# Spatial gating g of a two-layer encoder step starts with U(g+1) instead of U(g), and its first loads are issued during VM

## The chip, the core and the metric

The kernel runs on one core of a Trainium2 chip. The metric is the device time of one execution in microseconds (us). The engines are TensorE (PE, its weight loads PEld), VectorE (DVE), ScalarE (ACT) and SyncE (SP, which here issues every DMA). GpSimd (POOL) does nothing that matters.

## The reference, cut to what matters

Each of the two layers normalises x, multiplies it by one combined matrix `w_in`, and feeds two branches: retention (q, k, v, gr) and a gated MLP (u, vm, gm). Only the second matters here. There are 288 tokens: 256 of a prompt and 32 of a sample.

```
z = rmsnorm(x) @ w_in
q, k, v, gr, u, vm, gm, ar, am = split(z)
u  = gelu(u)
vn = layernorm(gelu(vm), ln_g, ln_b)          # over all 2048 channels: needs the whole of vm
s  = einsum(W_s, vn) + bias                   # per group of 256 channels, mixes positions
m_branch = (silu(gm) * u * s) @ w_mlp_out
merged = sigmoid(ar) * r_branch + sigmoid(am) * m_branch
x = x + merged @ w_o
```

## The kernel before

**Jobs and pieces.** Every projection is cut into jobs of 256 output channels, and a job into four pieces (`KP` = 4 k-tiles of 128 x 256 weights, 512 KB). All operands are split into a high and a low fp32r part, and a product takes three matmuls (`mm3`, lines 111 to 113), so that a piece is 4 x 2 x 3 = 24 matmuls. A layer has 88 jobs: first eight of VM (pieces 0 to 31 of the layer), then, before the change, U0, GM0, U1, GM1 ... U7, GM7 (pieces 32 to 95), then AM0, AM1, W_MLP0 and so on. Below, "piece 42" or "step 42" counts within a layer.

**What a step emits.** The order on every engine is the order in which the main loop (line 769) writes the instructions; nothing reorders them later. At step s it emits the high part of piece s+4 (`emit_hi`: ACT, tile `whi`, 5 buffers), the low part of piece s+3 (`emit_lo`: DVE, tile `wlo`, 4 buffers, so that DVE can write it only when PE has finished piece s-1), the load of piece s+7 (`emit_raw`: SP, tile `raw`, 4 buffers), the job's `pre` function if it is a first piece, the 24 matmuls, and then one `tick()`. A tick advances every active generator by one `yield`: the evacuations (`evac_*`, started after the last piece of their job) and the spatial gatings (`sgu_gen`, started in `pre`). I call the tick of step 37 "tick 37".

**Spatial gating.** `sgu_gen(l, g)` waits until the layer norm's statistics are there (`state["ln"]`, written in tick 37 by the last VM evacuation). Then, tick by tick: it clears a part of `wr` (DVE, line 292, which needs that matrix loaded) and normalises one of three token blocks of `vmt` (tile `vmacc`, lines 299 and 301), ACT takes the high part of the matrix (tile `wsp`, one buffer); then DVE takes the low parts and does the other two blocks; then ACT writes `vh`, and SP gets the store `out_gv` and, through `load_sgu`, the five loads of gating g+1 (480 KB: `ln_g`, `ln_b`, `ws_b`, `ws`, `ws_s`); then DVE writes `vl` and the low part of `vh` (line 108); then PE does ten matmuls (lines 324 to 326), and DVE adds the bias and multiplies by u (lines 328 to 332, tile `rqh`). `evac_gm(g)` multiplies the result by silu(gm). The loads of gating 0 are issued by gating 0's own first step, at piece 32.

Before the change gating 0 starts with U0 at piece 32 but waits for the statistics, and gating 1 starts with U1 at piece 40; so the two run side by side from tick 40 on.

Of the kernel before, what the change touches and what calls it, by code (L numbers as in the profile page):

```python
# [23 lines left out]
NPR = DM // 256  # L24
# [6 lines left out]
Q0, K0, V0, GR0, U0, VM0, GM0, AR0, AM0 = 0, 4, 8, 16, 24, 32, 40, 48, 56  # L31
# [11 lines left out]
def trunk(ctx: ExitStack, tc: tile.TileContext, a, o):  # L43
# [9 lines left out]
    def st(shape, tag, dt=F32, bufs=1):  # L53
        return sb.tile(shape, dt, tag=tag, name=tag, bufs=bufs)

    def aux():
        return psx.tile([P, 512], F32, tag="aux", name="aux")
# [19 lines left out]
    def load(dst, src):  # L77
        nc.sync.dma_start(out=dst, in_=src)  # L78
# [25 lines left out]
    def to_hi(src, hi):  # L104
        S.copy(out=hi, in_=src)  # L105

    def to_lo(src, hi, lo):
        V.tensor_tensor(out=lo, in0=src, in1=hi.bitcast(F32), op=ALU.subtract)  # L108
# [125 lines left out]
    def halves2(p):  # L234
        return p.rearrange("p (j c) -> p j c", j=2)
# [31 lines left out]
    def load_sgu(l, g):  # L267
        if g == NPR:
            return
        lg, lb = st([P, 416], "c0", bufs=2)[:, 0:256], st([P, 256], "c1", bufs=2)  # L270
        load(lg, a["ln_g"][l, g].partition_broadcast(P))
        load(lb, a["ln_b"][l, g].partition_broadcast(P))
        bs = st([P, 384], "wh", bufs=2)[:, 0:T]
        load(bs, a["ws_b"][l, g].partition_broadcast(P))
        wr = st([P, P], "wsr", bufs=2)
        load(wr, a["ws"][l, g])
        wq = st([P, TS], "wsq", bufs=2)
        load(wq, a["ws_s"][l, g])
        state["sgu", g] = (lg, lb, bs, wr, wq)

    def sgu_gen(l, g):
        if g == 0:
            load_sgu(l, 0)
        lg, lb, bs, wr, wq = state.pop(("sgu", g))
        while "ln" not in state:
            yield
        if g == 0:
            yield
        vmt, r = state["vmt"], state["ln"]
        if g == NPR - 1:  # L290
            state.pop("ln")
        V.memset(wr[64:128, 0:64], 0.0)
        w2 = st([P, 2, P], "wsp", F32R)
        to_hi(wr, w2[:, 0])
        wsk = st([P, TS], "wsk", F32R, bufs=2)
        to_hi(wq, wsk)
        for b in range(3):
            x = vmt[:, g, :, b]
            V.scalar_tensor_tensor(out=x, in0=x, scalar=mvl[:, b, 0:1], in1=halves2(lg),  # L299
                                   op0=ALU.subtract, op1=ALU.mult)  # L300
            V.scalar_tensor_tensor(out=x, in0=x, scalar=r[:, b:b + 1], in1=halves2(lb),
                                   op0=ALU.mult, op1=ALU.add)
            if b == 0:
                yield
                to_lo(wr, w2[:, 0], w2[:, 1])
                for q in ODD:
                    to_lo(wq[q], wsk[q], wsk[q])
        yield
        vh, vl = st([P, 2, 3, P], "vh", F32R, bufs=2), st([P, 2, 2, P], "vl", F32R, bufs=2)
        to_hi(vmt[:, g], vh)  # L310
        load(halves2(o["gv"][l, :, g * 256:g * 256 + 256]), vmt[0:TS, g, :, 2])
        load_sgu(l, g + 1)
        yield
        to_lo(vmt[:, g, :, 0:2], vh[:, :, 0:2], vl)
        to_lo(vmt[HALF, g, :, 2], vh[HALF, :, 2], vh[HALF, :, 2])
        yield
        while ("u", g) not in state:
            yield
        sg = st([P, 2, T], "rqh")
        ps_ = aux()  # L320
        for d in range(2):
            p = aux().rearrange("p (b h i) -> p b h i", b=2, h=2)
            for b in range(2):
                PE.matmul(p[:, b], vh[:, d, b], w2, start=True, stop=False)  # L324
                PE.matmul(p[:, b, 0], vl[:, d, b], w2[:, 0], start=False, stop=True)  # L325
            PE.matmul(ps_[:, d * TS:d * TS + TS], vh[:, d, 2], wsk, start=True, stop=True)
            x = sg[:, d, 0:TP].rearrange("p (b i) -> p b i", b=2)
            V.tensor_tensor(out=x, in0=p[:, :, 1], in1=bs[:, 0:TP].rearrange("p (b i) -> p b i", b=2), op=ALU.add)  # L328
            V.tensor_tensor(out=x, in0=p[:, :, 0], in1=x, op=ALU.add)
        V.tensor_tensor(out=sg[:, :, TP:T], in0=ps_[:, 0:2 * TS].rearrange("p (d i) -> p d i", d=2),  # L330
                        in1=bs[:, TP:T].unsqueeze(1).to_broadcast([P, 2, TS]), op=ALU.add)
        V.tensor_tensor(out=sg, in0=sg, in1=state.pop(("u", g)), op=ALU.mult)
        state["s", g] = sg

    def evac_u(l, g, ps):
        z = scaled(ps, "zu", 2)
        S.activation(out=z, in_=z, func=AF.Gelu)
        yield
        state["u", g] = z
# [280 lines left out]
    for l in range(DEPTH):  # L620
        A, B = ("A", "B") if l % 2 == 0 else ("B", "A")
        hs, mg, rg, mr = Set(A), Set(B), Set(B), Set(A)
        sets[l] = (hs, mg, rg, mr)

        def job(pair, ops, fn, c, pre=None, l=l):
            jobs.append((l, pair, ops, fn, c, pre))

        for c in range(NPR):
            job(VM0 + c, hs, evac_vm, c)
        for g in range(NPR):  # L630
            job(U0 + g, hs, evac_u, g, lambda l, g: start(sgu_gen(l, g)))
            job(GM0 + g, hs, evac_gm, g)
        job(AM0, hs, evac_am, 0)
        for c in range(NPR):
            if c + 1 < NPR:
                job(AM0 + c + 1, hs, evac_am, c + 1)
            job(W_MLP + c, mg, evac_mlp, c)
        for hp in range(H // 2):
            job(Q0 + hp, hs, evac_q, hp, pre_q)
            job(K0 + hp, hs, evac_k, hp)  # L640
            for jj in range(2):
                job(V0 + 2 * hp + jj, hs, evac_v, 2 * hp + jj)
            for jj in range(2):
                job(GR0 + 2 * hp + jj, hs, evac_gr, 2 * hp + jj)
        for c in range(NPR):
            job(AR0 + c, hs, evac_ar, c)
        for c in range(NPR):
            job(W_RET + c, rg, evac_ret, c)
        for c in range(NPR):
            job(W_O + c, mr, evac_o, c, pre_o)  # L650
# [39 lines left out]
    def start(gen):  # L690
        active.append(gen)
# [77 lines left out]
    for s, (j, i) in enumerate(pieces):  # L769
        l, pair, ops, fn, c, pre = jobs[j]  # L770
# [6 lines left out]
        if i == 0:  # L777
# [5 lines left out]
            hs, mg, rg, mr = sets[l]  # L783
# [133 lines left out]
```

## Time and profile before

| what | us |
|---|---|
| median of three runs | 2361.43 |
| lowest, highest | 2360.75, 2362.48 |
| the profiled execution, own time | 2362.0 |
| its span (first to last instruction) | 2360.2 |
| PE busy | 2335.9 (99%) |
| DVE busy | 1424.1 (60%) |
| ACT busy | 1020.2 (43%) |
| mean granted TensorE clock | 0.995 |

PE is busy nearly all the time, so that a change of order can only win or lose the stretches in which PE waits, or in which it runs at the lower of its two clock levels. The rows are to be read with the engine that waits first, and what it waited for second.

### The profile page before, as it was taken

To read this page: it belongs to the slowest core of one execution; us is meant where nothing else is said; L and a number is where in the kernel's file an instruction comes from. 1 tells how busy PE (TensorE), PEld (TensorE's weight loads), DVE (VectorE), ACT (ScalarE), POOL (GpSimd) and SP (SyncE) were. 2 spreads that over 40 slices of the span, in tenths; PEclk is the share of its full clock that TensorE was granted. 3 is DMA by queue.
4 is the path that set the end of the run, shared out by engine and by line. 5 is a ranking of instruction groups with operands and counts; after the bars stand their busy time and mean duration, and the time that the engine had idled before them with its cause. 6 is when DMAs were issued, how large, how long until landed. Compare 5 with 4: busy or idle time off the path is not lost.

```text
span 2360.2 us, 42693 instructions
## 1 busy us (share of the span) xinstructions
PE 2335.9 (99%) x17572; PEld 2333.9 (99%) x17572; DVE 1424.1 (60%) x2145; ACT 1020.2 (43%) x1298; POOL 0.2 (0%) x4
## 2 busy tenths in 40 slices
PE   9999999999999999999999999999999999999997
PEld 9999999999999999999999999999999999999997
DVE  7567764446777774455555777544467777645554
ACT  6445543333444453334444445433344444433342
POOL 0000000000000000000000000000000000000000
PEclk9999999999999999999999999999999999999999
DMA  8855554556778785456688555445577877744553
GB/s 268 234 171 180 175 173 163 168 165 185 219 206 230 201 223 173 163 168 193 210 218 229 165 176 177 163 163 168 172 203 198 222 206 212 219 164 162 169 196 115
DMA packets 350164, 446.36 MB, mean 189 GB/s; under 512 B 193552, under 2 KB 254736, under 8 KB 349968
## 3 DMA queue, kind: packets, MB, share of 16 engines
q1 hardware_dynamic: 349968, 443.63, 62.1%
q8 instruction: 138, 2.26, 0.4%
q14 instruction: 58, 0.48, 0.1%
HBM read 412.09 MB, written 31.46 MB: 188 GB/s over the span
## 4 chain that ended last, share of the span: by engine, by line
PE 96%; DVE 2%; issue 1%; DMA 1%; SPq 0%; ACT 0%; DVEq 0%; ACTq 0%
PE ps L111 31%; PE ps L112 31%; PE ps L113 31%; PE aux L112 1%; PE aux L113 1%; PE aux L111 1%; DMA raw<-in_w_in 1%; PE aux L324 0%; DVE wlo L108 0%; DMA vmacc<-zd 0%; SPq L78 0%; PE aux L325 0%; DVE vmacc L825 0%; DVE vmacc L299 0%; PE aux L423 0%
## 5 line engine op out<-in xcount | busy, mean ns | idle before, releaser
L108 DVE TENSOR_TENSOR wlo<-raw,whi 128x1024 fp32r<-128x1024 f32 (+1 forms) x705 | 858.0, 1218 | 509.3 <-PE ps L113 321.5
L105 ACT CAST whi<-raw 128x1024 fp32r<-128x1024 f32 (+1 forms) x705 | 733.2, 1047 | 817.8 <-PE ps L112 659.1
L111 PE MATMUL ps<-Ah,whi 128*128 128x288 f32 x2816 | 832.6, 296 | 1.4 <-ACT whi L105 1.4
L113 PE MATMUL ps<-Ah,wlo 128*128 128x288 f32 x2816 | 832.0, 295 | 0.7 <-DVE wlo L108 0.7
L112 PE MATMUL ps<-Al,whi 128*128 128x288 f32 x2816 | 831.2, 295 | 0.0
L111 PE MATMUL ps<-Bh,whi 128*128 128x288 f32 x2784 | 825.2, 296 | 0.0
L112 PE MATMUL ps<-Bl,whi 128*128 128x288 f32 x2784 | 823.8, 296 | 0.0
L113 PE MATMUL ps<-Bh,wlo 128*128 128x288 f32 x2784 | 823.8, 296 | 0.0
L111 PEld LDWEIGHTS ps<-Ah,whi 128*128 128x128 f32 x2816 | 529.8, 188 | 1.9 <-ACT whi L105 1.9
L113 PEld LDWEIGHTS ps<-Ah,wlo 128*128 128x128 f32 x2816 | 529.3, 188 | 1.4 <-DVE wlo L108 1.4
L112 PEld LDWEIGHTS ps<-Al,whi 128*128 128x128 f32 x2816 | 529.1, 188 | 0.0
L112 PEld LDWEIGHTS ps<-Bl,whi 128*128 128x128 f32 x2784 | 524.4, 188 | 0.0
L111 PEld LDWEIGHTS ps<-Bh,whi 128*128 128x128 f32 x2784 | 523.9, 188 | 0.0
L113 PEld LDWEIGHTS ps<-Bh,wlo 128*128 128x128 f32 x2784 | 523.4, 188 | 0.0
L209 DVE TENSOR_TENSOR z<-ps,rsb 128x576 f32<-128x576 f32 x52 | 39.3, 755 | 61.7 <-PE ps L113 61.7
L512 ACT ACTIVATE on<-aux,gnb,gny 128x256 f32<-128x256 f32 x48 | 23.6, 562 | 65.4 <-DVE gnb L508 65.4
L216 DVE STREAM_TRANSPOSE zt<-ps 128x512 f32<-128x512 f32 x32 | 22.9, 715 | 39.8 <-PE ps L113 38.2
L503 DVE BATCH_NORM_STATS2 gst<-aux 128x6 f32<-128x256 f32 x48 | 17.5, 421 | 34.5 <-PE aux L113 34.5
L355 ACT ACTIVATE z<-z 128x576 f32<-128x576 f32 x16 | 11.0, 687 | 46.3 <-DVE z L209 46.3
L384 DVE TENSOR_TENSOR zu<-ps,cosr 128x576 f32<-128x576 f32 x16 | 12.1, 758 | 30.6 <-PE ps L113 30.6
L375 DVE TENSOR_TENSOR vmacc<-ps,z 128x576 f32<-128x576 f32 x16 | 12.1, 758 | 30.6 <-PE ps L113 30.6
L328 DVE TENSOR_TENSOR rqh<-aux,wh 128x256 f32<-128x256 f32 x32 | 13.4, 419 | 27.8 <-PE aux L325 27.8
(221 smaller groups left out, 1146.1 us busy)
## 6 DMA issues: line engine op xcount, KB each, us to landing
raw<-in_w_in SPq DMA_DIRECT2D x511, 512.0 KB, 4.7
raw<-in_w_mlp SPq DMA_DIRECT2D x64, 512.0 KB, 4.6
raw<-in_w_ret SPq DMA_DIRECT2D x64, 512.0 KB, 4.6
raw<-in_w_o SPq DMA_DIRECT2D x64, 512.0 KB, 4.6
zd<-zt SPq DMA_DIRECT2D x224, 96.0 KB, 3.7
vmacc<-zd SPq DMA_DIRECT2D x56, 384.0 KB, 5.8
c<-in_dmask SPq DMA_DIRECT2D x16, 208.0 KB, 4.8
vmacc<-in_x SPq DMA_DIRECT2D x8, 288.0 KB, 6.8
```

The source lines that it names most:

```text
L105: S.copy(out=hi, in_=src)
L108: V.tensor_tensor(out=lo, in0=src, in1=hi.bitcast(F32), op=ALU.subtract)
L111: PE.matmul(out, lh, rh, start=start, stop=False)
L112: PE.matmul(out, lh, rl, start=False, stop=False)
L113: PE.matmul(out, ll, rh, start=False, stop=stop)
L209: V.tensor_tensor(out=z, in0=ps[:, :, 0:T], in1=bc2(state["rs"]), op=ALU.mult)
L216: V.transpose(out=zt[:, :, 0:8], in_=src[:, :, 0:TP].rearrange("p j (b t) -> p j b t", t=TS))
L328: V.tensor_tensor(out=x, in0=p[:, :, 1], in1=bs[:, 0:TP].rearrange("p (b i) -> p b i", b=2), op=ALU.add)
L375: V.tensor_tensor(out=state["acc"][:, c], in0=ps[:, :, 0:T], in1=state.pop(("sig", c)), op=ALU.mult)
L384: V.tensor_tensor(out=r, in0=ps[:, :, 0:T], in1=bc2(cr), op=ALU.mult)
L503: V.bn_stats(out=bst[:, b], in_=src[b])
L512: S.activation(out=on[:, b], in_=src[b], func=AF.Identity, bias=nb[:, b:b + 1], scale=y[:, b:b + 1])
```

## The change

Gating g now starts in the `pre` of U(g+1) (gating 7 in that of GM7); the jobs stand in the order U0, U1, GM0, U2, GM1, ... U7, GM6, GM7, so that U1 has pieces 36 to 39, GM0 40 to 43 and U2 44 to 47. The five loads of gating 0 are issued in the `pre` of VM5 (piece 20) instead of at piece 32.

```diff
     def sgu_gen(l, g):
-        if g == 0:
-            load_sgu(l, 0)
         lg, lb, bs, wr, wq = state.pop(("sgu", g))
...
+    def pre_vm(l, c):
+        if c == 5:
+            load_sgu(l, 0)
+
+    def start_sgu(l, g):
+        if g:
+            start(sgu_gen(l, g - 1))
...
         for c in range(NPR):
-            job(VM0 + c, hs, evac_vm, c)
+            job(VM0 + c, hs, evac_vm, c, pre_vm)
         for g in range(NPR):
-            job(U0 + g, hs, evac_u, g, lambda l, g: start(sgu_gen(l, g)))
-            job(GM0 + g, hs, evac_gm, g)
+            job(U0 + g, hs, evac_u, g, start_sgu)
+            if g:
+                job(GM0 + g - 1, hs, evac_gm, g - 1)
+        job(GM0 + NPR - 1, hs, evac_gm, NPR - 1, lambda l, g: start_sgu(l, NPR))
         job(AM0, hs, evac_am, 0)
```

What this moves on the engines, at three places of layer 0 (layer 1 has the same rows). In the listings a row is a line of the program, an operation, and output<-inputs; line numbers above 280 differ between the two kernels by a few.

DVE, from the evacuation after piece 39 on. Before: `z` is GM0's result, the first `wlo` is that of step 40, the MEMSET and the two rows under it (with the tiles `c_1676`, `c_1677`) are the start of gating 1, the second `wlo` is that of step 41, and `vl`, `vh` are gating 0's low parts.

```order
L209 TENSOR_TENSOR z<-ps,rsb 128x576
L108 TENSOR_TENSOR wlo<-raw,whi 128x1024
L292 MEMSET wsr 64x64
L299 SCALAR_TENSOR_TENSOR vmacc<-vmacc,mvl,c_1676 128x2x128
L301 SCALAR_TENSOR_TENSOR vmacc<-vmacc,lny,c_1677 128x2x128
L108 TENSOR_TENSOR wlo<-raw,whi 128x1024
L108 TENSOR_TENSOR vl<-vmacc,vh 128x512
L108 TENSOR_TENSOR vh<-vmacc,vh 64x2x128
```

The same place on DVE in the changed kernel (`zu` is U1's result).

```order
L209 TENSOR_TENSOR zu<-ps,rsb 128x576
L108 TENSOR_TENSOR wlo<-raw,whi 128x1024 x2
L108 TENSOR_TENSOR vl<-vmacc,vh 128x512
L108 TENSOR_TENSOR vh<-vmacc,vh 64x2x128
L108 TENSOR_TENSOR wlo<-raw,whi 128x1024
L326 TENSOR_TENSOR rqh<-aux,wh 128x256
```

The three rows of gating 1 no longer stand ahead of gating 0's `vl` and `vh`; they now stand behind gating 0's bias and product rows, in step 44. On PE, gating 0's ten matmuls stand at the same place as before, behind piece 42; gating 1's stand behind piece 48 instead of piece 45.

ACT, from the high part of piece 43 (step 39) on, before: `z` is GM0's silu, and the `wsp`, `wsk` rows are gating 1's.

```order
L105 CAST whi<-raw 128x1024
L343 ACT_TABLE_LOAD
L343 ACTIVATE z<-z 128x576
L105 CAST whi<-raw 128x1024
L105 CAST vh<-vmacc 128x768
L105 CAST wsp<-wsr 128x128
L105 CAST wsk<-wsq 128x32
L105 CAST whi<-raw 128x1024 x2
```

The same place on ACT in the changed kernel: `zu` is U1's gelu.

```order
L105 CAST whi<-raw 128x1024
L343 ACTIVATE zu<-zu 128x576
L105 CAST whi<-raw 128x1024
L105 CAST vh<-vmacc 128x768
L105 CAST whi<-raw 128x1024 x3
L349 ACT_TABLE_LOAD
L349 ACTIVATE z<-z 128x576
```

Gating 1's `wsp` moved behind GM0's silu, and U1's gelu follows U0's without a table load between them. Over the program, ACT's table loads for gelu and silu of U and GM go from 30 to 26.

SP, from the four stores of VM4's transposed result (`zd<-zt`) on, before.

```order
L78 DMA zd<-zt 32x24x32 x4
L78 DMA raw<-in_w_in 128x1024 x2
L78 DMA vmacc<-zd 128x6x128
L78 DMA raw<-in_w_in 128x1024 x2
```

The same place on SP in the changed kernel.

```order
L78 DMA zd<-zt 32x24x32 x4
L78 DMA raw<-in_w_in 128x1024
L78 DMA c_937<-in_ln_g 128x256
L78 DMA c_938<-in_ln_b 128x256
L78 DMA wh<-in_ws_b 128x288
L78 DMA wsr<-in_ws 128x128
L78 DMA wsq<-in_ws_s 128x32
L78 DMA raw<-in_w_in 128x1024
L78 DMA vmacc<-zd 128x6x128
```

The five loads moved here from the same position three jobs later (behind VM7's stores and one `raw`).

## Rows read from the trace of the kernel before

**Rows 1.** The page: the span, and busy time, share and instructions by engine.

```profile
span 2360.2 us, 42693 instructions
PE 2335.9 (99%) x17572; PEld 2333.9 (99%) x17572; DVE 1424.1 (60%) x2145; ACT 1020.2 (43%) x1298; POOL 0.2 (0%) x4
```

**Rows 2.** Waits of PE: who waited for whom, total us, times, longest.

```profile
PE aux L325 <- DVE vl L108: 9.0, 2, 5.6
```

**Rows 3.** Timeline of PE, layer 0: start, duration, instruction, [idle before <-releaser].

```profile
146.92 0.28 PE L324 MATMUL aux<-wsp,vh 128*128 128x256 f32 x1
152.77 0.47 PE L325 MATMUL aux<-wsp,vl 128*128 128x128 f32 x1 [5.57 <-DVE vl L108]
...
157.72 0.30 PE L111 MATMUL ps<-Ah,whi 128*128 128x288 f32 x1
...
165.68 0.28 PE L324 MATMUL aux<-wsp,vh 128*128 128x256 f32 x1
...
168.42 0.30 PE L111 MATMUL ps<-Ah,whi 128*128 128x288 f32 x1
...
192.32 0.28 PE L324 MATMUL aux<-wsp,vh 128*128 128x256 f32 x1
```

**Rows 4.** Timeline of PE, layer 1, the same place.

```profile
1314.96 0.28 PE L324 MATMUL aux<-wsp,vh 128*128 128x256 f32 x1
1318.67 0.47 PE L325 MATMUL aux<-wsp,vl 128*128 128x128 f32 x1 [3.42 <-DVE vl L108]
...
1325.07 0.30 PE L111 MATMUL ps<-Bh,whi 128*128 128x288 f32 x1
```

**Rows 5.** Windows: us, busy (instructions) by engine, granted clock, DMA share, GB/s.

```profile
60.00:100.00 40.00, 40.00 (x303) 40.00 (x303) 21.13 (x29) 17.12 (x22) 0.00 (x0) 1.00 0.92 248
152.80:157.70 4.90, 4.90 (x21) 4.90 (x22) 2.81 (x9) 2.31 (x4) 0.00 (x0) 0.50 0.31 107
1318.70:1325.00 6.30, 6.30 (x27) 6.30 (x28) 4.21 (x10) 2.32 (x4) 0.00 (x0) 0.50 0.25 83
```

**Rows 6.** Timeline of DVE: layer 0, gating 2 of layer 0, layer 1.

```profile
129.25 1.23 DVE L108 TENSOR_TENSOR wlo<-raw,whi 128x1024 fp32r<-128x1024 f32 x1 [2.55 <-ACT whi L105]
...
141.25 1.22 DVE L108 TENSOR_TENSOR wlo<-raw,whi 128x1024 fp32r<-128x1024 f32 x1
149.83 0.11 DVE L292 MEMSET wsr<- 64x64 f32 x1 [7.36 <-DMA wsr<-in_ws]
...
152.03 0.68 DVE L108 TENSOR_TENSOR vl<-vmacc,vh 128x512 fp32r<-128x512 f32 x1
152.74 0.42 DVE L108 TENSOR_TENSOR vh<-vmacc,vh 64x256 fp32r<-64x256 f32 x1
...
184.87 0.42 DVE L108 TENSOR_TENSOR vh<-vmacc,vh 64x256 fp32r<-64x256 f32 x1
...
1315.72 0.11 DVE L292 MEMSET wsr<- 64x64 f32 x1 [6.51 <-DMA wsr<-in_ws]
```

**Rows 7.** Timeline of ACT: layer 0, then layer 1.

```profile
141.96 1.04 ACT L105 CAST whi<-raw 128x1024 fp32r<-128x1024 f32 x1
142.90 0.83 ACT L105 CAST vh<-vmacc 128x768 fp32r<-128x768 f32 x1
154.82 0.30 ACT L105 CAST wsp<-wsr 128x128 fp32r<-128x128 f32 x1 [11.09 <-PE aux L325]
...
1308.71 1.03 ACT L105 CAST whi<-raw 128x1024 fp32r<-128x1024 f32 x1
1309.64 0.83 ACT L105 CAST vh<-vmacc 128x768 fp32r<-128x768 f32 x1
```

**Rows 8.** Timeline of SP's queue: the load of gating 1's matrix.

```profile
144.81 0.38 SPq L78 DMA_DIRECT2D wsr<-in_ws  x1
```

**Rows 9.** Chain that ended last, in order of time: start, us, what.

```profile
118.58 9.49 DMA raw<-in_w_in
```

**Rows 10.** Groups by line, ACT: xcount, busy us, mean ns, idle before.

```profile
L343 ACT ACT_TABLE_LOAD x16 | 20.5, 1283 | 0.3
```

## The prediction

> **What bounds the kernel now.** I read the page first: PE is busy 2335.9 of 2360.2 us [rows 1], so nothing that DVE, ACT or SP win counts unless PE waits for it. Next the waits of PE: the longest by far is on the low part `vl` in front of a spatial gating's matmuls, 9.0 us in two waits [rows 2]. The timeline of PE puts them at gating 0 of each layer: it comes to the gating's first matmul at 146.92 and to the one that reads `vl` only at 152.77, idle 5.57 us [rows 3]; in layer 1 the wait is 3.42 us [rows 4]. The other fourteen gatings show none.
>
> The wait is dearer than its idle time. Behind both waits the windows show a granted clock of 0.50, for 4.9 and 6.3 us [rows 5]: the engine had sat idle, and then ran at 1.2 GHz instead of 2.4.
>
> Who made `vl` late? On DVE the low part of piece 43 starts at 141.25 and takes 1.22 us. Then DVE stands at gating 1's MEMSET until 149.83, waiting 7.36 us for that gating's matrix [rows 6], whose load SP had issued only at 144.81 [rows 8]. `vl` is queued behind it and comes at 152.03. ACT had `vh` ready at 142.90 + 0.83 = 143.73 [rows 7], so DVE alone was late. ACT too stood still there, 11.09 us before gating 1's `wsp` [rows 7], since that tile has one buffer, which gating 0's matmuls still had to read: a loop of gating 1 blocking gating 0. Layer 1 shows the same DVE wait, 6.51 us [rows 6].
>
> **The change part by part.**
>
> *The stall's price.* In layer 0 the stretch from the gating's first matmul to the first one back at full clock is 157.72 - 146.92 = 10.80 us and holds ten gating matmuls and twelve of a piece. Gating 1 does the same 22 in 168.42 - 165.68 = 2.74 us [rows 3]. So the stall costs 8.06 us (5.57 idle, and half of the 4.9 us at half clock, 2.45, make 8.02). In layer 1 the stretch is 1325.07 - 1314.96 = 10.11 us [rows 4] with eighteen piece matmuls. At full clock sixty of them take 165.68 - 157.72 = 7.96 us [rows 3], 0.133 each, so undisturbed it is 2.74 + 6 x 0.133 = 3.54, and the stall costs 6.57 us (3.42 + 6.3/2 = 6.57). Together 14.6 us.
>
> *Does the move remove it?* In the changed order DVE's queue goes from `wlo` of step 40 straight to `wlo` of step 41, `vl` and `vh`. PE's own order up to gating 0 is unchanged, so PE still comes to it at 146.92. When is `vl` there? `wlo` of step 41 needs the high part of piece 44, which ACT ends at 141.96 + 1.04 = 143.00 [rows 7], a buffer that piece 40 gave back (PE ends piece 40 two pieces of 24 x 0.133 = 3.18 us before 146.92, at 140.56), and DVE, which is free at 142.47. So: 143.00 + 1.22 (`wlo`) + 0.68 (`vl`) + 0.42 (`vh`) = 145.3, with the durations of [rows 6]: 1.6 us before PE. In layer 1: 1308.71 + 1.03 + 1.22 + 0.68 + 0.42 = 1312.1 [rows 6, 7] against 1314.96 [rows 4]: 2.9 us. What is late next is nothing on PE's side: the margin is there, but not wide. From below, a stall that stays in part costs its idle time and up to 3.15 us of half clock; I take all 14.6 as won, since every row in that sum is one measured in the place itself.
>
> *Gating 1's wait.* Its rows are still loaded by the same five DMAs at about 144.8, and were usable at 149.83 [rows 6, 8]. DVE now comes to the MEMSET in step 44, behind a `wlo` that waits for PE to end piece 43: 146.92, plus the block (2.74 - 12 x 0.133 = 1.15), plus 3.18, is 151.25, plus 1.22 is 152.5. So the rows are there 2.6 us before they are wanted. And PE wants the result behind piece 48, 148.07 + 6 x 3.18 = 167.1. ACT's wait for `wsp` goes too: gating 0's matmuls are two steps back by then.
>
> *Gatings 1 to 7.* Each now starts four pieces before its matmuls instead of five, so PE asks one piece sooner. For gating 2, `vh` was done at 184.87 + 0.42 = 185.3 [rows 6] and PE came at 192.32 [rows 3]; one piece sooner is 189.1, which leaves 3.8 us. Cost nothing; if the cover went, each of the fourteen would cost what it is late.
>
> *The loads of gating 0.* Five DMAs, 480 KB, move on SP's queue past three jobs' stores, reads and raw pieces, from piece 32 to piece 20. VM is the stretch where the DMA engines are fullest, a share of 0.92 at 248 GB/s [rows 5], so they push 480/248 = 1.9 us of traffic ahead of one raw piece and one `vmacc` read. The nearest row is the same push at VM7: the raw piece behind it landed after 9.49 us [rows 9], ACT was late, and DVE waited 2.55 us for it until 129.25 [rows 6]. That `wlo` (piece 40) was done at 130.48, and PE came to piece 40 at 146.92 - 3 x 3.18 = 137.4: 6.9 us to spare. So I take nothing for it; below zero it can't go, as PE waited for nothing there before. At VM7 the relief can bring the statistics earlier by up to those 2.55 us, which only widens the 1.6 us margin.
>
> *Instruction counts* are the same on PE, DVE and SP. ACT has four table loads fewer, of 1.283 us [rows 10]. They lie before a gelu or silu whose input comes later from DVE, so I take nothing for them.
>
> **The sum.** Against the profiled execution's own 2362.0 us (span 2360.2, 1.8 around it): 2362.0 - 14.6 = 2347.4. That execution lies 0.6 above the median of the runs shown, so the median should go to 2346.8, 0.62% less.
>
> **The rivals.**
>
> *A remnant of the stall.* For it: the 1.6 us in layer 0 hang on ACT's high part of piece 44, and DVE has come out of a dense stretch. Against: every row is measured in place, and the relief at VM7 helps. If ACT is 2.5 to 4 us later, PE idles 1 to 2.5 us and pays 0 to 3.15 us at half clock: 1 to 5.6 us, so 2348 to 2352.5; in both layers at most 2358.
>
> *The wait only moves.* If DVE still meets a load that has not landed in front of `vl` (the step at fault being the order, or U1's evacuation taking the place of the blocked row), PE waits as before: 2361.4. The order of DVE speaks against it.
>
> *Starved in VM (slower than before).* The five loads are issued where the DMA engines have least room, once per layer. If the raw piece behind them lands later than 9.49 + 6.9 = 16.4 us after its issue, PE waits for its low part. To end on the slow side that must eat 14.6 us: 7.3 per layer, say 4.8 idle and 2.5 at half clock, from a landing of 21 us; at 24 us it is 7.6 + 2.5 to 3.15, about 10.5 per layer, so 2346.8 + 21 = 2368. The 1.9 us of traffic speaks against it.
>
> *ACT's table loads count.* If ACT were in the way wherever it switches tables, four loads less would give another 4 x 1.283 = 5.1 us: 2341.7. PE's wait in that stage is on DVE [rows 2], not on ACT, so hardly. The Trainium skill, ScalarE: Activation LUTs, section What ACT_TABLE_LOAD costs, puts the same 1283 ns on the load, with which [rows 10] agrees, and about 1.4 us of draining on top; by it the four switches would be worth some 10.6 us (an estimate from that page), which no row here shows.
>
> **How the numbers follow.** Forecast 0.81, remnant 0.11, wait only moves 0.03, starved 0.03, table loads 0.02. The half-clock stretches differed by 1.4 us between the layers, worth 0.7, and the runs spread by 0.7 below and 1.1 above their median; so the forecast alone is 2345 to 2348.5. I reach up to 2353 to take in a remnant in one layer, which leaves out about one in ten. About 0.2% (4.7 us) is what a measurement of this kernel can tell from no change: faster than 2356.7 are the forecast, the table loads and nearly all remnants, 0.93; within 0.2% the moved wait and the worst remnants, 0.04; slower 0.03.
>
> **What would show it.** Right: PE's waits no longer name `vl`; the granted clock stays at 1.00 around 147 to 158 and 1315 to 1325; DVE's `vh` of gating 0 ends near 145 and 1312; the MEMSET of gating 1 has no DMA in front of it, near 152.5; PE's busy time falls by some 5 us, its idle time by 9. Wrong: any idle of PE before a gating's matmuls, a wait of PE on `wlo` or `whi` between pieces 20 and 32, or a clock below 1.00 in either place.

## The result and the profile after

The changed kernel takes 2347.93 us (median of four runs, 2347.08 to 2348.91) against 2361.95 us of the kernel before in the same comparison (four runs). The ratio is 0.9941, with a 95% interval of 0.9924 to 0.9959: 14.0 us less. The forecast was 2346.8, in a range of 2345.0 to 2353.0.

The page of the changed kernel: PE is busy 4.4 us less than in [rows 1], and its idle time (span less busy) fell from 24.3 to 14.5 us, near the 5 and 9 us less that the prediction looked for.

```profile
span 2346.0 us, 42689 instructions
PE 2331.5 (99%) x17572; PEld 2329.9 (99%) x17572; DVE 1424.6 (61%) x2145; ACT 1016.0 (43%) x1294; POOL 0.2 (0%) x4
```

The waits of PE in the changed kernel, longest first (total us, times, longest). The row of [rows 2] is gone; what is left lies at the start and the end of the program.

```profile
PE aux L188 <- DVE z L98: 2.8, 1, 2.8
PE aux L726 <- DVE ones L720: 1.0, 1, 1.0
PE ps L113 <- DVE wlo L108: 1.0, 2, 0.7
```

The timeline of PE at gating 0 of layer 0 and of layer 1, as in [rows 3, 4]: the matmul that reads `vl` follows the first one after 0.12 us, and the pieces go on 1.06 us after the gating's first matmul.

```profile
147.28 0.28 PE L322 MATMUL aux<-wsp,vh 128*128 128x256 f32 x1
147.40 0.22 PE L323 MATMUL aux<-wsp,vl 128*128 128x128 f32 x1
...
148.34 0.38 PE L111 MATMUL ps<-Ah,whi 128*128 128x288 f32 x1
...
1307.25 0.28 PE L322 MATMUL aux<-wsp,vh 128*128 128x256 f32 x1
1307.37 0.22 PE L323 MATMUL aux<-wsp,vl 128*128 128x128 f32 x1
```

The windows (us, busy by engine, granted clock, DMA share, GB/s) behind gating 0 of both layers and in the stretches where [rows 5] had 0.50: 1.00 everywhere.

```profile
146.90:152.80 5.90, 5.90 (x49) 5.90 (x48) 4.63 (x9) 2.54 (x3) 0.00 (x0) 1.00 0.87 227
152.80:157.70 4.90, 4.90 (x39) 4.90 (x38) 4.75 (x9) 3.37 (x6) 0.00 (x0) 1.00 0.64 204
1300.00:1314.00 14.00, 14.00 (x109) 14.00 (x108) 10.84 (x16) 8.12 (x9) 0.00 (x0) 1.00 0.65 188
1314.00:1325.00 11.00, 11.00 (x85) 11.00 (x84) 9.45 (x18) 6.40 (x9) 0.00 (x0) 1.00 0.57 179
```

The timeline of DVE, as in [rows 6]: `vl` and `vh` follow the two `wlo`, and gating 1's MEMSET comes ten microseconds later, with no idle time before it. So the MEMSET that had to wait for a load no longer stands in front of `vl`.

```profile
140.40 1.22 DVE L108 TENSOR_TENSOR wlo<-raw,whi 128x1024 fp32r<-128x1024 f32 x1
142.18 1.23 DVE L108 TENSOR_TENSOR wlo<-raw,whi 128x1024 fp32r<-128x1024 f32 x1 [0.56 <-ACT whi L105]
143.32 0.69 DVE L108 TENSOR_TENSOR vl<-vmacc,vh 128x512 fp32r<-128x512 f32 x1
144.04 0.42 DVE L108 TENSOR_TENSOR vh<-vmacc,vh 64x256 fp32r<-64x256 f32 x1
...
154.43 0.11 DVE L290 MEMSET wsr<- 64x64 f32 x1
```

**Where the 14 us went.** The two profiles can be cut at PE's first matmul of gating 0 in each layer. Between the two marks the kernel before took 1314.96 - 146.92 = 1168.04 us, the changed one 1307.25 - 147.28 = 1159.97: 8.07 less. From the second mark to the end of the span it was 2360.2 - 1314.96 = 1045.24 and 2346.0 - 1307.25 = 1038.75: 6.49 less. Up to the first mark the changed kernel took 0.36 longer, which is within the spread of the start (in the twelve profiles of the table below the mark lies between 146.92 and 148.76). Together 14.2 us of span.

### The profile page after: what moved, and what is told of

Same layout as the page of the kernel before. It is cut to its first block, busy times and chain, and to the rows that moved or that the text cites. A ratio compares the mean times of both kernels' runs of the same rounds, so it can differ in the third digit from the quotient of the medians.

```text
span 2346.0 us, 42689 instructions
## 1 busy us (share of the span) xinstructions
PE 2331.5 (99%) x17572; PEld 2329.9 (99%) x17572; DVE 1424.6 (61%) x2145; ACT 1016.0 (43%) x1294; POOL 0.2 (0%) x4
## 4 chain that ended last, share of the span: by engine, by line
PE 99%; DVE 0%; DMA 0%; SPq 0%; ACT 0%; issue 0%; DVEq 0%
PE ps L111 32%; PE ps L112 32%; PE ps L113 32%; PE aux L112 1%; PE aux L113 1%; PE aux L111 1%; PE aux L322 0%; DMA raw<-in_w_in 0%; DVE vmacc L833 0%; PE aux L323 0%; SPq L78 0%; PE aux L429 0%; PE aux L180 0%; PE aux L324 0%; PE aux L522 0%; PE aux L503 0%
```

## The experiments

The same cut serves for every run. PE does the same work in all of them, so what a run takes over 1159.97 and 1038.75 is the cost of what went wrong in that layer. "Idle" is PE's wait on gating 0's `vl`. The stretches come from one profiled execution of each kernel, the medians from all its runs; each ratio below is against the kernel before in the same comparison (medians 2360.89 to 2361.95). The five kernels without a disturbance (changed, e2, e4, x4, e8) agree in both stretches to within 0.09 us.

| kernel | PE at gating 0, layers 0 and 1 | span | idle, layers 0, 1 | cost, layers 0, 1 | median of the runs |
|---|---|---|---|---|---|
| before | 146.92, 1314.96 | 2360.2 | 5.57, 3.42 | 8.07, 6.49 | 2361.95 |
| changed | 147.28, 1307.25 | 2346.0 | 0, 0 | 0, 0 | 2347.93 |
| e1_loads_only | 147.91, 1314.61 | 2360.1 | 4.37, 3.36 | 6.73, 6.74 | 2361.79 |
| e2_order_only | 148.76, 1308.73 | 2347.4 | 0, 0 | 0.00, -0.08 | 2347.64 |
| e3_rows_early | 147.99, 1309.66 | 2348.9 | 0.79, 0 | 1.70, 0.49 | 2350.89 |
| e4_start_only | 147.14, 1307.11 | 2345.8 | 0, 0 | 0.00, -0.06 | 2347.76 |
| y1_split_early | 147.23, 1307.74 | 2347.0 | 0, 0 | 0.54, 0.51 | 2348.76 |
| y2_both_in_vm | 147.89, 1308.41 | 2347.9 | 0, 0 | 0.55, 0.74 | 2349.13 |
| x4_spare | 147.01, 1306.99 | 2345.7 | 0, 0 | 0.01, -0.04 | 2347.79 |
| x7_idle | 147.47, 1309.43 | 2351.6 | 1.59, 1.51 | 1.99, 3.42 | 2353.73 |
| x10_idle | 147.36, 1314.28 | 2360.1 | 3.77, 3.68 | 6.95, 7.07 | 2360.85 |
| e8_push_960 | 148.12, 1308.09 | 2346.8 | 0, 0 | 0.00, -0.04 | 2348.42 |

### Which part of the change does it

The change has three parts: the loads of gating 0 at VM5, the later start of each gating, and the order of the jobs.

**e1_loads_only** takes the first part alone.

```diff
     def sgu_gen(l, g):
-        if g == 0:
-            load_sgu(l, 0)
...
+    def pre_vm(l, c):
+        if c == 5:
+            load_sgu(l, 0)
...
-            job(VM0 + c, hs, evac_vm, c)
+            job(VM0 + c, hs, evac_vm, c, pre_vm)
```

> The kernel before, with only the five loads of gating 0 moved to VM5; job order and start of the gatings as before. Theory (gating 1's rows, not gating 0's, hold vl up): DVE still stands at gating 1's MEMSET for its matrix, up to 2.5 us longer in layer 0 since it may get there earlier; PE still waits 5.6 and 3.4 us before vl and then runs at half clock; time within 3 us of the kernel before, 2359 to 2364. Rival (the late loads of gating 0 made the statistics and so vl late): half or more of the 14 us comes back, 2355 or less.

Measured: 2361.79 us, ratio 1.0003, interval 0.9994 to 1.0011: no change. Its timeline of DVE has the same two waits for gating 1's matrix, its timeline of PE the idle time behind them. The wait of layer 0 is 1.2 us shorter than the forecast 5.6, and that stall 1.3 us cheaper, but the median does not show it.

```profile
149.61 0.11 DVE L290 MEMSET wsr<- 64x64 f32 x1 [7.36 <-DMA wsr<-in_ws]
...
1315.30 0.11 DVE L290 MEMSET wsr<- 64x64 f32 x1 [6.43 <-DMA wsr<-in_ws]
```

```profile
152.55 0.47 PE L323 MATMUL aux<-wsp,vl 128*128 128x128 f32 x1 [4.37 <-DVE vl L108]
...
1318.24 0.47 PE L323 MATMUL aux<-wsp,vl 128*128 128x128 f32 x1 [3.36 <-DVE vl L108]
```

So the early loads of gating 0 are worth nothing measurable by themselves.

**e2_order_only** takes the other two parts without the first.

```diff
     def pre_vm(l, c):
-        if c == 5:
-            load_sgu(l, 0)
+        pass
     def start_sgu(l, g):
         if g:
             start(sgu_gen(l, g - 1))
+        else:
+            load_sgu(l, 0)
```

> The changed kernel with gating 0's loads issued at U0 (piece 32) as before the change; only job order and start of the gatings changed. Theory: the whole gain is here, no PE wait on vl, 2347 to 2349; vl and the low part of vh end near 145 in layer 0, some 1 us later than in the changed kernel, since the raw piece behind the loads lands late again. Rival (the early loads carry part of it, the margin in layer 0 being too small without them): a remnant of 1 to 6 us, 2349 to 2354.

Measured: 2347.64 us, ratio 0.9945, interval 0.9932 to 0.9957: the whole gain. `vl` ended 144.80 + 0.69 = 145.5 with PE at the gating at 148.76, so that it was as far ahead of PE as in the changed kernel (143.32 + 0.69 = 144.0 with 147.28). The early loads brought nothing forward here.

**e4_start_only** keeps the old order of the jobs and starts gating g with GM(g).

```diff
-            job(U0 + g, hs, evac_u, g, lambda l, g: start(sgu_gen(l, g)))
-            job(GM0 + g, hs, evac_gm, g)
+            job(U0 + g, hs, evac_u, g, lambda l, g: g == 0 and load_sgu(l, 0))
+            job(GM0 + g, hs, evac_gm, g, lambda l, g: start(sgu_gen(l, g)))
```

> The kernel before with its job order U0, GM0, U1, GM1 ... kept, but gating g started with GM(g), four pieces later than before; gating 0's loads at U0. ACT has all 30 table loads for gelu and silu (26 in the changed kernel). Theory: as good as the changed kernel, 2347 to 2349, because only the start of gating 1 behind gating 0 counts. Rival (the job order matters, by the four table loads or by GM0's evacuation waiting on ACT or DVE): 1 to 6 us more, 2349 to 2354.

Measured: 2347.76 us, ratio 0.9944, interval 0.9931 to 0.9956, and the same two stretches as the changed kernel to within 0.06 us. It has all 30 table loads for gelu and silu; this is its group of them for silu in the groups by line (count, busy us, mean ns, idle before).

```profile
L341 ACT ACT_TABLE_LOAD x16 | 20.5, 1283 | 0.3
```

It differs from e2_order_only (2347.64 us) only in the order of the jobs, and with that in the four table loads. So neither counts. The later start of the gatings is the part that gains.

### What of the early start cost so much

Gating 1 started early put two things ahead of gating 0's `vl`: a wait for rows that had not landed, and three rows of DVE work (and on ACT a `wsp` that waits for PE). **e3_rows_early** takes the first away and leaves the second.

```diff
     def sgu_gen(l, g):
         if g == 0:
             load_sgu(l, 0)
+            load_sgu(l, 1)
...
-        load_sgu(l, g + 1)
+        if g:
+            load_sgu(l, g + 1)
```

> The kernel before, with gating 1's five loads issued together with gating 0's at piece 32, some 22 us earlier; job order, start of the gatings and the order of DVE and ACT as before. Theory A (the DMA wait alone made vl late): no DMA wait before the MEMSET; wlo 142.5, three rows of gating 1 to 143.6, wlo, vl, vh to about 146.0, before PE comes at 146.9; gain as in the changed kernel, 2347 to 2350, though ACT still waits for wsp some 4 us. Theory B (gating 1 standing ahead of gating 0 on DVE and ACT is what costs): PE still waits some us, 2352 to 2360.

Measured: 2350.89 us, ratio 0.9957, interval 0.9944 to 0.9971: between the two theories. The wait for the rows is gone, but `vl` of layer 0 is late all the same, and PE waits 0.79 us. In order: ACT, DVE, PE of this run, and last the same ACT row in the kernel before.

```profile
131.76 1.05 ACT L105 CAST whi<-raw 128x1024 fp32r<-128x1024 f32 x1 [4.40 <-DMA raw<-in_w_in]
```

```profile
148.32 0.69 DVE L108 TENSOR_TENSOR vl<-vmacc,vh 128x512 fp32r<-128x512 f32 x1
```

```profile
149.06 0.33 PE L327 MATMUL aux<-wsp,vl 128*128 128x128 f32 x1 [0.79 <-DVE vl L108]
```

```profile
128.17 1.05 ACT L105 CAST whi<-raw 128x1024 fp32r<-128x1024 f32 x1 [1.88 <-DMA raw<-in_w_in]
```

ACT's wait for its raw piece had grown from 1.88 to 4.40 us: the piece stands on SP behind the ten loads, 960 KB at piece 32, and behind it on ACT stand the last VM gelu and so the statistics. So the run left open whether the remnant came from that traffic or from gating 1's work standing first. Two more runs tell these apart; both keep job order and start as before, and change only when the rows of gatings 0 and 1 are loaded. **y1_split_early**: gating 0's at VM5, gating 1's at U0. **y2_both_in_vm**: gating 0's at VM5, gating 1's at VM6. (The pieces of code are those of e1 and e3, with `load_sgu(l, 1)` in U0's `pre`, or in `pre_vm` at c == 6.)

> The kernel before, job order and start of the gatings kept; gating 0's five loads at VM5 and gating 1's at U0 (piece 32), so that no more than 480 KB go ahead of one raw piece. Theory A (in the run with both sets at piece 32 the remnant came from the 960 KB there, which held up the raw piece and with it the statistics): vl ends at about 146.0 in layer 0 before PE comes at 147, no PE wait on vl, 2347 to 2349. Theory B (gating 1's rows ahead of gating 0's on DVE and its wsp on ACT make the remnant): a wait of PE on vl of 0.5 us or more stays, 2350 or more.

> The kernel before, job order and start of the gatings kept; gating 0's loads at VM5, gating 1's at VM6 (piece 24), none at piece 32. Theory A: statistics some 1 to 2.5 us earlier than in the kernel before, vl ends near 145 although gating 1's three rows (1.1 us) and a table load still stand where they stood, no PE wait, 2347 to 2348.5, as the changed kernel. Theory B (order of the gatings counts): 2350 or more.

Measured: y1 2348.76 us, ratio 0.9947, interval 0.9933 to 0.9960, as theory A has it; y2 2349.13 us, ratio 0.9948, interval 0.9936 to 0.9960, which is 0.6 us above theory A's range and below theory B's. The timeline of DVE, y1 first, then y2; PE comes to gating 0 of layer 0 at 147.23 and 147.89 and does not wait.

```profile
145.46 0.69 DVE L108 TENSOR_TENSOR vl<-vmacc,vh 128x512 fp32r<-128x512 f32 x1
```

```profile
144.51 0.68 DVE L108 TENSOR_TENSOR vl<-vmacc,vh 128x512 fp32r<-128x512 f32 x1
```

So nearly all of the gain is had without touching the order, by loading gating 1's rows in time: the wait for them was the cause. Of e3's remnant, 1.70 and 0.49 us in the two layers, y1 and y2 keep 0.5 to 0.7 us per layer. What they lose of it, 1.2 us in layer 0, was the traffic of the 960 KB in one place.

What stays is a delay of gating 1, where gating 1's earlier start still costs something. In y1 PE comes to gating 1 at 157.93 and goes on with the pieces at 159.53, 1.60 us later, where the same block of gating 0 took 1.06 us in the changed kernel. The difference is the whole 0.54 us of layer 0. The matmul that reads `vl` starts when `vl` is done, at 157.57 + 0.69 = 158.26.

```profile
157.93 0.28 PE L323 MATMUL aux<-wsp,vh 128*128 128x256 f32 x1
158.31 0.33 PE L324 MATMUL aux<-wsp,vl 128*128 128x128 f32 x1
...
159.53 0.38 PE L111 MATMUL ps<-Ah,whi 128*128 128x288 f32 x1
```

```profile
148.78 0.29 DVE L108 TENSOR_TENSOR wsp<-wsr,wsp 128x128 fp32r<-128x128 f32 x1 [2.19 <-ACT wsp L105]
...
157.57 0.69 DVE L108 TENSOR_TENSOR vl<-vmacc,vh 128x512 fp32r<-128x512 f32 x1
```

DVE had waited 2.19 us for gating 1's `wsp`, whose one buffer ACT could write only behind gating 0's matmuls, and from 148.78 on it worked without a pause up to this `vl`. So the loop through `wsp` that the prediction names holds up gating 1 and not gating 0. That a second buffer would end the delay was not tried.

This half microsecond lies below what the medians can tell (the intervals overlap with the changed kernel's); it is read from the profiles alone.

### How much room there is, and what an idle PE costs

Three runs compute gating 0's `vl` several times over, in the changed kernel, which puts known work ahead of PE.

```diff
-        to_lo(vmt[:, g, :, 0:2], vh[:, :, 0:2], vl)
+        for _ in range(5 if g == 0 else 1):      # 8 and 11 in the other two
+            to_lo(vmt[:, g, :, 0:2], vh[:, :, 0:2], vl)
```

> The changed kernel with gating 0's vl computed five times instead of once (four repeats of 0.68 us on DVE, 2.7 us, in each layer). In the changed kernel vl ends at 144.0 in layer 0 and PE reads it at 147.40, 3.4 us later. Theory (a spare of 3.4 us): the repeats are hidden, vl ends at 146.7, no PE wait, 2347 to 2349. Rival (spare smaller, since the next wlo and its buffers are late too): a wait and 1 to 5 us more.

> The changed kernel with gating 0's vl computed eight times (seven repeats, 4.8 us on DVE, in each layer). Theory: vl ends at 148.8, PE idles 1.4 us in layer 0 and 0 to 1 in layer 1; whether the clock falls after so short an idle is open: if not, 1 to 2.5 us over the changed kernel, 2349 to 2350.5; if it does, up to 6 us more, 2351 to 2356.

> The changed kernel with gating 0's vl computed eleven times (ten repeats, 6.8 us on DVE, in each layer). Theory: PE idles 3.4 us in layer 0 and 2.5 to 3.4 in layer 1 and runs at half clock for 4 to 7 us after each, as the kernel before did after 3.42 us; 6 to 6.7 us per layer, 2359 to 2362. Rival (the idle alone counts): 6 to 7 us in all, 2354 to 2355.

Measured: x4 2347.79 us, ratio 0.9943, interval 0.9926 to 0.9960: four repeats are hidden. x7 2353.73 us, ratio 0.9969, interval 0.9957 to 0.9981, in the range given for a clock that falls; the idle time in layer 1 was 1.51 us, where 0 to 1 was expected. x10 2360.85 us, ratio 0.9997, interval 0.9988 to 1.0007: all of the gain is lost again, with 7.5 us of idle time where the kernel before had 9.0. The five computations of x4 on DVE:

```profile
143.06 3.60 DVE L108 TENSOR_TENSOR vl<-vmacc,vh 128x512 fp32r<-128x512 f32 x5
```

The waits of PE in x7, one in each layer, and the granted clock in the windows behind them. It stayed at 1.00 in layer 0, and in layer 1 it was at the lower level between 1313 and 1315:

```profile
149.34 0.33 PE L324 MATMUL aux<-wsp,vl 128*128 128x128 f32 x1 [1.59 <-DVE vl L108]
...
1311.22 0.33 PE L324 MATMUL aux<-wsp,vl 128*128 128x128 f32 x1 [1.51 <-DVE vl L108]
```

```profile
149.00:155.00 6.00, 5.66 (x43) 5.61 (x44) 5.84 (x11) 0.93 (x1) 0.00 (x0) 1.00 0.58 177
...
1313.00:1315.00 2.00, 2.00 (x10) 2.00 (x9) 1.90 (x6) 0.00 (x0) 0.00 (x0) 0.50 0.54 135
1311.00:1318.00 7.00, 6.78 (x40) 6.74 (x41) 5.97 (x11) 0.89 (x1) 0.00 (x0) 0.76 0.37 116
```

And in x10, the wait of layer 0 and the windows behind both waits:

```profile
151.41 0.47 PE L324 MATMUL aux<-wsp,vl 128*128 128x128 f32 x1 [3.77 <-DVE vl L108]
```

```profile
151.00:157.00 6.00, 5.59 (x24) 5.59 (x25) 5.54 (x10) 0.00 (x0) 0.00 (x0) 0.50 0.29 89
...
1318.20:1324.00 5.80, 5.76 (x25) 5.76 (x26) 5.19 (x9) 0.00 (x0) 0.00 (x0) 0.51 0.29 90
```

The same in e1_loads_only:

```profile
152.60:157.00 4.40, 4.40 (x19) 4.40 (x20) 2.34 (x7) 2.31 (x4) 0.00 (x0) 0.50 0.38 119
...
1318.20:1324.00 5.80, 5.75 (x25) 5.76 (x26) 3.69 (x9) 2.32 (x4) 0.00 (x0) 0.50 0.30 90
```

The table has six waits of 3.36 to 5.57 us (before, e1 and x10). Behind each of them the clock was granted at 0.50 or 0.51, and the layer lost 2.4 to 3.4 us on top of the idle time (in x10 6.95 and 7.07 us for 3.77 and 3.68 of idle, a little over the 6 to 6.7 that were expected). Behind the two waits of 1.5 to 1.6 us it fell in one layer and not in the other.

### Is there room for the loads in VM

**e8_push_960** issues gating 1's rows at VM5 as well, in the changed kernel (`load_sgu(l, 1)` beside `load_sgu(l, 0)`, and none at gating 0's own step).

> The changed kernel with gating 1's five loads issued at VM5 too, so that 960 KB instead of 480 go ahead of one raw piece where the DMA engines are fullest. Theory (6.9 us to spare): the raw piece lands some 2 us later still, DVE's low part is later by as much, PE waits for nothing between pieces 20 and 32; 2347 to 2349, as the changed kernel. Rival (VM has no room): PE waits for wlo there, 2350 or more, and the clock falls below 1.00 behind the wait.

Measured: 2348.42 us, ratio 0.9945, interval 0.9930 to 0.9960, and PE waits for nothing in VM. The traffic is felt, but not by PE. The waits of ACT for raw pieces between 70 and 130 us (total, times, longest), the changed kernel first, then e8; the kernel before had 4.4 us in two.

```profile
ACT whi L105 <- DMA raw<-in_w_in: 22.1, 10, 4.4
```

```profile
ACT whi L105 <- DMA raw<-in_w_in: 32.0, 13, 7.5
```

The low part of piece 28 on DVE, changed kernel and e8:

```profile
91.16 1.23 DVE L108 TENSOR_TENSOR wlo<-raw,whi 128x1024 fp32r<-128x1024 f32 x1 [2.08 <-ACT whi L105]
```

```profile
95.85 1.23 DVE L108 TENSOR_TENSOR wlo<-raw,whi 128x1024 fp32r<-128x1024 f32 x1 [5.92 <-ACT whi L105]
```

PE comes to piece 28 fifteen pieces of 3.18 us before the gating's matmuls: at 147.28 - 47.8 = 99.5 in the changed kernel and 100.3 in e8. The low part was done at 92.4 and 97.1. So 7.1 us were left with 480 KB and 3.2 us with 960 KB.

## Why the prediction was right, point by point

- **What bounds the kernel, and why `vl` was late.** Held. The wait for gating 1's rows is the cause: e1 keeps it and keeps the time, y1 and y2 remove it alone and have all but 0.8 and 1.2 us of the gain. ACT's wait for `wsp`, which the prediction names beside it, stays in y1 and y2 and makes the half microsecond per layer that they lack, not the stall.
- **The stall's price.** 8.06 and 6.57 us were forecast; the cut of the profiles gives 8.07 and 6.49. This was the term that carried the number, and it was right because it compared the disturbed stretch with the same work undisturbed, instead of counting the idle time (9.0 us).
- **Whether the move removes it.** Held. Forecast: the low part of `vh` done 1.6 us before PE comes in layer 0, 2.9 in layer 1. Measured: 2.8 us (144.46 and 147.28) and 2.9 us. So layer 1 was right, and in layer 0 the margin was undersized by 1.2 us: I had started from ACT's high part of piece 44 as it stood in the kernel before, where the statistics were themselves 1.2 us late. `vl` alone, which PE reads first, is there 3.4 us ahead, and x4 put 2.9 us (3.60 - 0.69) in there at no cost. I ascribed such a relief to the loads leaving VM7. The runs are divided on that: with them gone `vl` comes 1.2 us earlier against PE in e1 than in the kernel before, but e2, which leaves them there, has the whole margin, and e4, which leaves them there too, all but 0.3 us of it. So how late they make the statistics differs from one execution to the next.
- **Gating 1's wait.** Held in effect, missed in the number: the MEMSET came at 154.43, not 152.5, because I left out GM0's evacuation and its product, which stand ahead of it on DVE. The rows were there either way.
- **Gatings 1 to 7 and table loads at nothing.** Held: e4, with other places and all the table loads, has the same two stretches.
- **The loads in VM at nothing.** Held, and the 6.9 us of spare, taken from VM7, is the 7.1 us read at VM5. The traffic was underrated in one respect: ACT's waits for raw pieces rose from 4.4 to 22.1 us, in ten waits up to 130 us, where I had counted one late piece.
- **The rivals.** The remnant did not come, but it exists as a mechanism at about the price I gave it: in x7 1.59 us of idle time cost 1.99 us and 1.51 cost 3.42. Starvation in VM was not reached with twice the load, which left 3.2 us. The moved wait and the table loads did not show.

Left open: why the clock fell behind one idle time of 1.5 us and not behind the other could not be told from these profiles, and the 0.36 us at the start is taken as spread, not explained.

## What to carry to other kernels

When an in-order engine waits for a load in front of something urgent, look at who put that wait there: here it belonged to the next unit of work, started too early, and starting it four pieces later or loading its rows sooner gave the same gain to within 1.2 us. Price a stall of TensorE by the same work undisturbed elsewhere in the trace, since the time lost behind it comes on top: here 2.4 to 3.4 us for idle times of 3.4 to 5.6 us. Before moving transfers into a fuller stretch, take the spare of the work behind them from a place where the same push already happens.

## What the runs showed that I had not expected

Two idle times of PE of the same length did not cost the same: in x7, 1.59 us in layer 0 left the clock at 1.00 and cost 1.99 us, and 1.51 us in layer 1 was followed by a granted clock of 0.76 on average over the window of 7 us shown, and cost 3.42 us. And the longer idle time was not the dearer one behind it: 5.57 us cost 2.5 us on top, 3.77 us cost 3.2 us.
